# A two-layer hybrid trunk on one core: decay rows in fewer transfers, a new instruction list for the second layer, and a shortened last block

## The chip, the cores and the metric

The kernel runs on one core of one Trainium2 chip. The metric is the device time of one execution in microseconds; lower is better. Before the change the median of three timed runs is 1061.02 us (1060.3 to 1061.82). Besides these there is one profiled execution, from which all rows of this document come.

## The reference

The program is one inference step of a trunk with two layers, on 128 prompt tokens and 512 sample tokens of width 1024, in float32. Each layer does a pre-RMSNorm, a shift and scale from a conditioning vector, a mixer branch and a gated residual add; a last RMSNorm follows. Layer 0's mixer is a convolution branch. Layer 1's mixer, where the whole change lies, is a bidirectional Mamba-2 scan:

```
u = h @ w_in
z, xbc, dt_raw = split(u)
xbc = silu(depthwise_conv(xbc, 5 taps))
xs, bm, cm = split(xbc)            # 32 heads of 64, 4 groups of state 128
dt = softplus(dt_raw + dt_bias)
y_f, s_f = ssd_scan(xs, dt_f, a_f, bm, cm, h0_f)              # chunks of 128 tokens
y_b, s_b = ssd_scan(flipped, ..., h0_b)
y = (y_f + flip(y_b) + d * xs) * silu(z)
y = rms_norm(y, per group of 512) * norm_g
out = y @ w_out
x = x + gate * out
result = rms_norm(x, final_norm_g)
```

Inside the scan each chunk needs the matrix `exp(a_cum[l] - a_cum[s])` (the decays) of each head, the product `C B^T`, and the states that are carried from chunk to chunk in both directions. The outputs are both token groups after the last norm, and the prompt's two final states.

## The kernel before

The 640 tokens are five chunks of 128: chunk 0 is the prompt, chunks 1 to 4 the sample. Each matrix product is split in three: activations and weights have a high and a low part in a reduced float32 format, and high by high, low by high and high by low are added in PSUM. So each weight tile is loaded (SyncE's queue, L1250), cast to its high part on ACT (L1255, or L1258 with the norm's gain folded in for the out-projection), and subtracted to its low part on DVE or POOL (L1264, L1267).

Nothing of the order is left to chance. The order of each engine's instructions is made by a list scheduler when the program is built (class `Order`, L247 and after). Work is written as generators that yield one operation at a time: its engine, an assumed duration, the call, and for a DMA the time that its bytes take. The scheduler keeps a clock for each engine and one for the transfers; it takes the operation that can start first, a priority from a table (`PRIO0` for layer 0, `PRIO1` for layer 1) breaking ties. A DMA with a byte time lands 0.3 us after its issue, plus the byte time, plus 2.2 us; TensorE's operations are placed `run.lead` after what they wait for. Ring buffers (`RB1`: xs, st, gf, gb and others) limit how far it can run ahead. What the scheduler decides is the order on each engine; on the chip the instructions wait for semaphores in that order. A wrong assumption therefore shows as an engine that waits while work behind it is ready.

Layer 1's backbone is `PLAN1`, a list of 45 tiles: x, b, c and z tiles of four groups (each 128 output columns over 640 tokens, 48 matmuls, L1307), and "o" pieces, the out-projection of a group's half (60 matmuls, L1558). Group 3's out-projection is not in the list: its weights come after the list's last tile (`out_weights`, L1862) and its products stand in `last_products` (L1901, matmuls L1913), which takes chunk after chunk, both halves of 512 columns, and starts a chunk only when all four weight tiles are there. After z33, the last z tile, SiLU (L1428, L1429), a gate product (L1787), a high and low split (L1811, L1816) and the sum of squares (L1829, L1833, L1834, L1839) stand before these products.

Between the layers, `first_steps` and `first_x` (L2084, L2093) empty the PSUM banks of the time steps and of the first two x tiles: most copies go to ACT (L1337, L1338, L2087, L2088).

The scan of a group (`group`, L1606) starts when B and all four x tiles of the group are there. For every chunk, `decays` (L1585) loads two tiles of decay rows from a table in DRAM that was written once: gb with 512 and gf with 1024 columns. The rows of the two directions come from different rows of the table, so partitions 0 to 63 and 64 to 127 have a transfer each: four transfers (L1599 twice, L1602 twice), each repeating one row of DRAM over 64 partitions. `decay` then subtracts on POOL (L1575), selects on DVE (L1577) and takes exponentials on ACT (L1581). Chunk states, their decay and their use are at L1633, L1638, L1652, L1666, L1701, L1705 and L1707; the products of decays and x at L1769.

The end: `last_residual` takes a product out of PSUM (L1924), adds it to x (L1927) and squares it with a running sum (L1928). `final` adds the sums of both halves (L1935), takes root and reciprocal (L1936, L1937); `final_half` scales and stores (L1951, L1953, L1955), `gained_half` has multiplied the first half by the norm's gain on POOL before (L1944).

Of the kernel before, what the change touches and what calls it, by code (L numbers as in the profile page):

```python
# [7 lines left out]
F32 = mybir.dt.float32  # L8
# [5 lines left out]
P = 128  # L14
# [29 lines left out]
PRIO1 = {"lead": -2, "sq_way": 2, "add_way": -3, "squares": -7, "room": -5, "roots": -2, "turn_x": 4, "gate_rows": 0, "gate_loads": -6, "residual": -5, "last_products": 3, "last_residual": 7, "final": 4, "gained_half": -5, "low": 1, "x_after": -4, "filler": 7, "decay_half": 5, "decay_state": 1, "chain0": -6, "chain1": 5, "other_y": 0, "copy_y": 7, "split_y": -1, "groups": 2, "decays": 0, "norms": 5, "gate": 6, "products1": 1, "products0": -7, "residual0": 0, "final0": -4, "w_chain": 3, "time_steps": 1, "columns": -5, "logarithm": 5, "rows_out": -3, "ends_out": 2, "weights_out": -6, "first_steps": 3, "b_after": 0, "c_after": 3, "z_after": -5, "split": 0, "add_residual": -5, "out_weights": -5, "free_bc": -4, "final1": -3, "prompt": -7, "residual1": 1, "store": 6, "final_rest": -4}  # L44
PLAN1 = "z00 b0 c0 z01 x02 x03 x13 b1 x10 x12 x22 x11 z02 x20 c1 x23 z03 b2 z10 x21 o00 z11 x33 o01 z12 z13 z20 c2 z30 x30 z21 x32 o10 z22 c3 z23 z31 o11 b3 x31 o20 z32 o21 z33"
RB1 = {"xs": 2, "st": 7, "gf": 2, "gb": 1}
# [5 lines left out]
def trunk(ctx: ExitStack, tc: tile.TileContext, a: dict):  # L52
# [1130 lines left out]
    if True:  # L1183
# [61 lines left out]
        def w_load(i, src, g=None):  # L1245
# [22 lines left out]

            def split():
                yield get("wh")  # L1270
# [29 lines left out]
        def dense_steps(ps, wh, wl, tiles, wofs, banks):  # L1300
# [12 lines left out]
        def project(i, name):  # L1313
            yield key(("w", i))
            yield get("mm")
            ps = mm(name)
            t = yield from dense_steps(ps, *W[i], h, [k * 128 for k in range(KD)], EVEN)
# [14 lines left out]
        def evacuate(ps):  # L1332

            ups.sort()
            u = up[ups.pop(0)[1]]
            if isinstance(ps, tuple):
                return u, tuple(lambda o=o, a0=a0, a1=a1: [S.copy(out=u[:, o + b * (a1 - a0) : o + (b + 1) * (a1 - a0)], in_=z_[:, a0:a1]) for b, z_ in enumerate(ps)] for o, a0, a1 in ((2, 0, 64), (132, 64, HN)))  # L1337
            return u, (lambda: S.copy(out=halves(u[:, 2:130]), in_=ps[:, :, 0:64]), lambda: S.copy(out=halves(u[:, 132:644]), in_=ps[:, :, 64:HN]))  # L1338

        def convolve(ps, j, tag, bufs, name, cell, u=None):  # L1340
            if u is None:
                yield get("up")
                u, copies = evacuate(ps)
                yield op(ACT, 0.27, copies[0])
                t = yield op(ACT, 0.6, copies[1])
# [150 lines left out]
        def gate_loads():  # L1496
            yield key(("gated",))
            for g in range(3):
                for hf in range(2):
# [7 lines left out]
                    t = yield op(SP, 0.9, load, 1.3)  # L1507
# [12 lines left out]
            t = yield op(SP, 1.8, load_last, 2.6)  # L1520
# [64 lines left out]
        def decays():  # L1585
            yield key(("cols",))
            for g in range(NG):
                for n, ch in enumerate(ORDER[g]):
# [4 lines left out]
                    def load():  # L1593
# [3 lines left out]
                        for i in range(2):  # L1597
                            r, col = at(1 - i, ch, 8 * g)
                            nc.sync.dma_start(out=gb[64 * i : 64 * i + 64], in_=acb[col // 128, i, r : r + 8, :].rearrange("h n -> (h n)").unsqueeze(0).broadcast_to([64, 512]))  # L1599
                        for i in range(2):  # L1600
                            r, col = at(i, ch, 8 * g)
                            nc.sync.dma_start(out=gf[64 * i : 64 * i + 64], in_=acf[col // 128, r : r + 8, :].rearrange("h n -> (h n)").unsqueeze(0).broadcast_to([64, 1024]))  # L1602
# [647 lines left out]
```

## Time and profile before

| what | value |
|---|---|
| timed runs, median (three) | 1061.02 us |
| the profiled execution's own time | 1060.24 us |
| its span, first to last instruction | 1058.3 us |
| mean granted TensorE clock | 0.995 |
| TensorE busy | 1032.8 us |
| VectorE (DVE) busy | 825.9 us |
| ScalarE (ACT) busy | 667.1 us |
| GpSimd (POOL) busy | 442.1 us |

The span is what the profile's rows count from and to; the execution's own time has 1.9 us around it. "Busy" of TensorE counts matmuls whose ends are modelled and which overlap, so 98% does not mean that the array works at its peak. Layer 1's first products of `PLAN1` start at 545.09 us, so the change concerns the second half of the span. A row of a chain or a timeline gives start and length in us, the engine, the line and the tiles; an "x" behind it is a count of instructions merged into it.

### The profile page before, as it was taken

The page shows a single profiled execution, that of the slowest core. Times are in us where ns is not written, and L with a number is a line of the kernel's source. Part 1 is how long each engine was busy: PE and PEld are TensorE (multiplying, and loading weights), DVE is VectorE, ACT ScalarE, POOL GpSimd, SP SyncE. Part 2 cuts the span into 40 slices and gives each one's busy share as a digit, 9 for nine tenths or more (in the row PEclk, how much of TensorE's full clock was granted, in tenths as well). Part 3 has the DMA queues.
Part 4 walks back from the last instruction along what each step waited for, and adds up shares of the span by engine and source line. Part 5 has one row for each costly group of instructions (what it writes and reads, how often), then busy time and mean ns, then how long its engine had stood idle before and what let it go on. Part 6 is the DMA issues. An engine that isn't in the chain of part 4 may idle for free.

```text
span 1058.3 us, 19181 instructions
## 1 busy us (share of the span) xinstructions
PE 1032.8 (98%) x7485; PEld 947.5 (90%) x7485; DVE 825.9 (78%) x1240; ACT 667.1 (63%) x1112; POOL 442.1 (42%) x443
## 2 busy tenths in 40 slices
PE   7999999999999999999999999999999999999986
PEld 4999999999999999999999988897879888998765
DVE  3589999998997689102678879889888687687897
ACT  6458788778687678433577666686556444572464
POOL 0029989978596511111000056334522644003642
PEclk9999999999999999999999999999999999999989
DMA  9598888788766667776222443334325344224513
GB/s 357 201 266 198 193 215 196 180 209 219 180 136 135 133 144 153 145 165 148 61 61 83 117 127 96 121 109 129 101 78 142 100 130 136 65 80 144 144 42 100
DMA packets 64362, 151.82 MB, mean 143 GB/s; under 512 B 9472, under 2 KB 22416, under 8 KB 64272
## 3 DMA queue, kind: packets, MB, share of 16 engines
q1 hardware_dynamic: 52480, 118.35, 36.0%
q0 software_dynamic: 8640, 30.94, 17.5%
q10 hardware_dynamic: 3152, 1.31, 0.5%
q8 instruction: 59, 0.97, 0.4%
q14 instruction: 31, 0.25, 0.1%
HBM read 145.45 MB, written 5.12 MB: 142 GB/s over the span
## 4 chain that ended last, share of the span: by engine, by line
PE 82%; DVE 6%; POOL 4%; ACT 4%; issue 2%; DMA 1%; SPq 1%; POOLq 0%; DVEq 0%; ACTq 0%
PE pz L1307 9%; PE xs L1307 8%; PE o L1558 8%; POOL cv L887 4%; PE o L1913 3%; PE po L1701 2%; PE B L1307 2%; PE C L1307 2%; PE pst L1638 2%; PE py L1769 2%; DVE cva L815 2%; PE o__4964 L158 1%; PE o__5273 L158 1%; PE o__5244 L158 1%; PE o__4954 L158 1%
## 5 line engine op out<-in xcount | busy, mean ns | idle before, releaser
L815 DVE SCALAR_TENSOR_TENSOR cva<-v,cst,cva 128x550 f32<-128x550 f32 (+12 forms) x346 | 270.3, 824 | 12.2 <-ACT cva L807 7.1
L887 POOL TENSOR_TENSOR cv<-cv,tp 128x490 f32<-128x490 f32 (+5 forms) x134 | 172.8, 1289 | 8.5
L846 ACT ACTIVATE tp<-v,cst 128x490 f32<-128x490 f32 (+5 forms) x134 | 92.5, 718 | 36.3 <-POOL cv L887 36.0
L425 ACT CAST wh<-wf 128x1024 fp32r<-128x1024 f32 x63 | 65.9, 1046 | 63.0 <-PE o__5273 L158 29.9
L1307 PE MATMUL pz<-h_hi,wh 128*128 128x320 f32 x256 | 86.3, 337 | 1.7 <-ACT up L1338 1.7
L1707 POOL TENSOR_TENSOR y<-y,yo 128x512 f32<-128x512 f32 x32 | 49.7, 1553 | 83.0 <-DVE yo L1705 79.3
L1307 PE MATMUL pz<-h_hi,wl 128*128 128x320 f32 x256 | 79.1, 309 | 0.0
L1307 PE MATMUL pz<-h_lo,wh 128*128 128x320 f32 x256 | 79.0, 309 | 0.0
L1307 PE MATMUL xs<-h_hi,wh 128*128 128x320 f32 x224 | 76.4, 341 | 0.0
L1351 DVE SCALAR_TENSOR_TENSOR xs<-up,cst,xs 128x642 f32<-128x642 f32 x64 | 65.7, 1028 | 10.2 <-ACT xs L1349 8.8
L1581 ACT ACTIVATE gf<-gf,cols 128x128 f32<-128x128 f32 x160 | 50.7, 391 | 29.8 <-DVE gf L1577 29.7
L1307 PE MATMUL xs<-h_hi,wl 128*128 128x320 f32 x224 | 69.3, 309 | 0.0
L1307 PE MATMUL xs<-h_lo,wh 128*128 128x320 f32 x224 | 69.1, 308 | 0.0
L435 ACT ACTIVATE wl<-wh 128x1024 fp32r<-128x1024 f32 x58 | 61.6, 1061 | 1.7
L1575 POOL TENSOR_TENSOR gb<-gb,cols 128x512 f32<-128x512 f32 x20 | 25.8, 1290 | 88.1 <-DMA gb<-acb 85.6
L1264 DVE TENSOR_TENSOR wl<-wf,wh 128x1024 fp32r<-128x1024 f32 x38 | 50.9, 1345 | 15.1 <-ACT wh L1255 15.1
L436 POOL DMA_DIRECT2D wl<-w_in x43 | 37.5, 872 | 54.8 <-ACT wl L435 54.2
L1307 PEld LDWEIGHTS pz<-h_hi,wh 128*128 128x128 f32 x256 | 48.1, 188 | 5.6 <-issue 3.4
L1558 PE MATMUL o<-wh,yh 128*128 128x512 f32 x120 | 53.2, 443 | 0.0
L1255 ACT CAST wh<-wf 128x1024 fp32r<-128x1024 f32 x38 | 39.6, 1047 | 18.1 <-DMA wf<-w_xbc 6.1
L1307 PEld LDWEIGHTS pz<-h_lo,wh 128*128 128x128 f32 x256 | 48.2, 188 | 3.1 <-issue 2.9
L436 POOL DMA_DIRECT2D wl<-w_out x15 | 13.0, 865 | 90.4 <-ACT wl L435 90.4
(848 smaller groups left out, 3500.4 us busy)
## 6 DMA issues: line engine op xcount, KB each, us to landing
wf<-w_in SPq DMA_DIRECT2D x48, 512.0 KB, 3.9
wl<-w_in POOLq DMA_DIRECT2D x43, 512.0 KB, 6.6
wa<-w_ada SPq DMA_DIRECT2D x64, 256.0 KB, 6.0
wf<-w_out SPq DMA_DIRECT2D x32, 512.0 KB, 3.6
wf<-w_xbc SPq DMA_DIRECT2D x24, 512.0 KB, 3.7
gf<-acf SPq DMA_DIRECT2D x40, 256.0 KB, 4.3
wa<-w_ada SPq DMA_DIRECT2D x16, 512.0 KB, 10.7
wf<-w_z SPq DMA_DIRECT2D x16, 512.0 KB, 3.7
```

What stands on the lines that cost most here:

```text
L425: t = yield op(ACT, 1.05, lambda: S.copy(out=wh, in_=wf))
L435: yield op(ACT, 1.06, lambda: S.activation(out=wl, in_=wh.bitcast(F32), func=AF.Copy, scale=-1.0))
L436: t = yield op(PD, 0.7, lambda: G.dma_start(out=wl, in_=src, accum_op=ALU.add))
L815: t = yield op(VE, 0.24 + 0.01 * (hi - lo), lambda: V.scalar_tensor_tensor(out=rows64(accs[i], lo, hi), in0=rows64(vs[i], lo + d, hi + d), ...
L846: t = yield op(ACT, 0.72, lambda: S.activation(out=tp[:, :, 0 : hi - lo], in_=rows64(vs[i], lo + d, hi + d), func=AF.Copy, scale=w_dw(i, t ...
L887: t = yield op(PO, 1.3 + 0.019 * (hi - lo - 49), lambda: G.tensor_add(out=rows64(cv[i], lo, hi), in0=rows64(cv[i], lo, hi), in1=sgs["tp", ...
L1264: e_.tensor_sub(out=cell["wl"], in0=cell["wf"], in1=cell["wh"].bitcast(F32))
L1307: T.matmul(ps[:, b, at_ : at_ + t1 - t0], lhsT=w_, rhs=t_[:, t0:t1], start=k == 0 and n == 0, stop=k == nk - 1 and n == 2)
L1351: t = yield op(VL, 0.97, lambda: V.scalar_tensor_tensor(out=acc, in0=u[:, d : d + PW], scalar=c("w_c", j * 5 + d), in1=acc, op0=ALU.mult, ...
L1558: T.matmul(ps, lhsT=t_, rhs=w_, start=k == 0 and n == 0, stop=k == 3 and n == 2)
L1581: t = yield op(ACT, 0.39, lambda: S.activation(out=gv[:, h_, :], in_=gv[:, h_, :], func=AF.Exp, bias=cols1[ch][:, o8 + h_ : o8 + h_ + 1]), ...
L1707: t = yield op(PO, 1.29, lambda: G.tensor_add(out=y, in0=y, in1=yo))
```

## The change

All of it lies in layer 1.

- **Tables.** `PLAN1`, `PRIO1` and `RB1` get new values. Two xs buffers become three, seven st buffers six.
- **Seam.** The first weight tile is cast in two halves, each subtracted on its own, and the first products of the first tile need the first half alone. The copies out of PSUM at the seam may go to DVE instead of ACT. The lead before TensorE's operations is 0.3 us up to the seam's end; after it `0.2 * (lead + 7)` with lead -4 (0.6 us) where it was -2 (1.0 us).
- **Decay rows.** Two transfers per chunk: one for gb and one for gf, each with a source pattern of two directions, times 64 repeats, times the row.
- **Landings.** The scheduler's byte times of several loads are changed: decays, gates, states and the chunk ends.
- **Late out-projection of group three.** Two of its four weight tiles are loaded with the list's weights and two by a generator of their own after z33. The products of each chunk and half are a chain of their own and need only that half's weights. The last chunk's second half is done in two pieces of 256 columns.
- **Final root.** The first sums are scaled and given epsilon ahead, and serve as the bias of the root.

```
-PLAN1 = "z00 b0 c0 z01 x02 x03 x13 b1 x10 x12 x22 x11 z02 x20 c1 x23 z03 b2 z10 x21 o00 z11 x33 o01 z12 z13 z20 c2 z30 x30 z21 x32 o10 z22 c3 z23 z31 o11 b3 x31 o20 z32 o21 z33"
-RB1 = {"xs": 2, "st": 7, "gf": 2, "gb": 1}
+PLAN1 = "x03 x02 x23 z00 b0 c0 z01 x10 b1 z02 x12 x13 z03 x11 x20 c1 z10 x21 c2 z11 x32 o00 x22 o01 z12 b2 z13 z20 c3 z21 x31 o10 z22 x30 o11 z23 x33 z30 b3 z31 o20 z32 z33 o21"
+RB1 = {"xs": 3, "st": 6, "gf": 2, "gb": 1}
...
             def split():
+                if i == 0:
+                    yield get("wh")
+                    yield get("wl")
...
+                    for n in range(2):
+                        t = yield op(ACT, 0.62, lambda: S.copy(out=cell["wh"][:, n * 512 : n * 512 + 512], in_=cell["wf"][:, n * 512 : n * 512 + 512]))
+                        start(first_half(n, t), t)
+                    return
...
                 for k, (hi, lo) in enumerate(tiles):
+                    if late and b == 0 and k == 4:
+                        yield key(late)
...
-                        for i in range(2):
-                            r, col = at(1 - i, ch, 8 * g)
-                            nc.sync.dma_start(out=gb[64 * i : 64 * i + 64], in_=acb[col // 128, i, r : r + 8, :].rearrange("h n -> (h n)").unsqueeze(0).broadcast_to([64, 512]))
-                        for i in range(2):
-                            r, col = at(i, ch, 8 * g)
-                            nc.sync.dma_start(out=gf[64 * i : 64 * i + 64], in_=acf[col // 128, r : r + 8, :].rearrange("h n -> (h n)").unsqueeze(0).broadcast_to([64, 1024]))
-                    t = yield op(SP, 1.5, load, 2.2)
+                        r, col = at(0, ch, 8 * g)
+
+                        def two(rows):
+                            v = rows.rearrange("(i p) n -> i p n", i=2)[:, r : r + 8, :].rearrange("i h n -> i (h n)")
+                            return v.unsqueeze(1).broadcast_to([2, 64, v.shape[1]])
+
+                        for t_, rows in ((gb, acb[col // 128].rearrange("f p n -> (f p) n")[64:192]), (gf, acf[col // 128])):
+                            nc.sync.dma_start(out=t_, in_=two(rows))
+                    t = yield op(SP, 1.1, load, 2.8)
...
-                t = yield op(SP, 0.45, load, 0.8)
+                t = yield op(SP, 0.45, load, 1.4)
...
+        def late_weights():
+            yield key(("z", 3, 3))
+            for n in range(2):
...
+                yield op(SP, 0.35, load, 1.35)
+                for k in range(2):
...
+                    yield op(ACT, 0.62, lambda: S.activation(out=wh, in_=wf, func=AF.Copy, scale=sn))
+                    t = yield op(VL, 0.72, lambda: V.scalar_tensor_tensor(out=wl, in0=wf, scalar=sn, in1=wh.bitcast(F32), op0=ALU.mult, op1=ALU.subtract))
...
-        def last_products():
-            for ch in LAST:
-                yield key(("split", 3, ch), *[("w3", n) for n in range(4)])
+        def last_products(ch, hf):
+            yield key(("split", 3, ch), ("w3", 2 * hf), ("w3", 2 * hf + 1))
...
+        def pieces(ch, hf):
+            return ((0, 256), (256, 512)) if (ch, hf) == (LAST[-1], 1) else ((0, 512),)
...
         def final(ch):
-            yield key(("fin", ch, 0), ("fin", ch, 1), ("fgb",))
-            r = fin[:, ch, 2:3]
-            yield op(VE, 0.15, lambda: V.tensor_add(out=r, in0=fin[:, ch, 0:1], in1=fin[:, ch, 1:2]))
-            yield op(ACT, 0.24, lambda: S.activation(out=r, in_=r, func=AF.Sqrt, scale=1.0 / 1024, bias=epsb), "sqrt")
+            r = fin[:, ch, 3:4]
+            n = len(pieces(ch, 1))
+            yield key(("fin", ch, 0, 0))
+            yield op(VE, 0.16, lambda: V.tensor_scalar(out=r, in0=fin[:, ch, 0:1], scalar1=1.0 / 1024, scalar2=EPS, op0=ALU.mult, op1=ALU.add))
+            if n > 1:
+                yield key(("fin", ch, 1, 0))
+                yield op(VE, 0.16, lambda: V.scalar_tensor_tensor(out=r, in0=fin[:, ch, 1:2], scalar=1.0 / 1024, in1=r, op0=ALU.mult, op1=ALU.add))
+            yield key(("fin", ch, 1, n - 1), ("fgb",))
+            yield op(ACT, 0.24, lambda: S.activation(out=r, in_=fin[:, ch, n : n + 1], func=AF.Sqrt, scale=1.0 / 1024, bias=r), "sqrt")
...
         def first_steps():
...
+                yield either((ACT, 0.27, lambda: take0(S)), (VE, 0.25, lambda: take0(V)), bias=0.1 * PRIO1["dt_way"])
...
         def first_x(j):
...
-            yield op(ACT, 0.27 + 0.2 * j, copies[0])
-            z_ = yield op(ACT, 0.6 + 0.2 * j, copies[1])
+            yield either((ACT, 0.27 + 0.2 * j, lambda: copies[0](S)), (VE, 0.25 + 0.15 * j, lambda: copies[0](V)), bias=0.1 * PRIO1["x_way"])
+            z_ = yield either((ACT, 0.6 + 0.2 * j, lambda: copies[1](S)), (VE, 0.67 + 0.1 * j, lambda: copies[1](V)), bias=0.1 * PRIO1["x_way"])
...
-            run.lead = 0.2 * (PRIO1["lead"] + 7)
+            run.lead = 0.3
...
             run.run(("begun",))
+            run.lead = 0.2 * (PRIO1["lead"] + 7)
...
-            start(last_products(), 0.0)
+            start(late_weights(), 0.0)
+            for ch in LAST:
+                for hf in range(2):
+                    start(last_products(ch, hf), 0.0)
```

More of the change, by code (lines that the diff above doesn't have):

```diff
@@ L1297, in w_free, with dense_steps @@
             put("wl", t)
-        def dense_steps(ps, wh, wl, tiles, wofs, banks):
+        def dense_steps(ps, wh, wl, tiles, wofs, banks, late=None):
             nk = len(tiles)
@@ L1316, in project @@
             ps = mm(name)
-            t = yield from dense_steps(ps, *W[i], h, [k * 128 for k in range(KD)], EVEN)
+            t = yield from dense_steps(ps, *W[i], h, [k * 128 for k in range(KD)], EVEN, None if i else ("w", 0, "b"))
             w_free(i, t)
@@ L1343, in convolve @@
                 u, copies = evacuate(ps)
-                yield op(ACT, 0.27, copies[0])
-                t = yield op(ACT, 0.6, copies[1])
+                yield op(ACT, 0.27, lambda: copies[0]())
+                t = yield op(ACT, 0.6, lambda: copies[1]())
                 put("mm", t)
@@ L1519, in load_last @@
                         gate_in(gts[3, hf][cd], cd, 4 * hf, 4)
[L1520 removed]
+            t = yield op(SP, 1.9, load_last, 4.2)
             post(("gt", 3), t)
@@ L1925, in last_residual, with as_x @@
             put("mm", t)
-            x_ = xv(ch, hf)
-            t = yield either((VL, 0.66, lambda: V.tensor_add(out=x_, in0=x_, in1=as_part(tmp, ch))), (PO, 1.29, lambda: G.tensor_add(out=x_, in0=x_, in1=as_part(tmp, ch))), bias=0.2)
-            t = yield op(ACT, 0.62, lambda: S.activation(out=as_part(tmp, ch), in_=x_, func=AF.Square, accum_out=fin[:, ch, hf : hf + 1]))
+            x_ = xs_[:, 4 * hf + c0 // 128 : 4 * hf + c1 // 128, :]
+            x_ = part(x_, ch)
+            def as_x(z_):
+                return z_.rearrange("p (j n) -> p j n", n=128) if half else as_part(z_, ch)
@@ L1929, in last_residual @@
+            if half:
+                t = yield op(VL, 0.42, lambda: V.tensor_add(out=x_, in0=x_, in1=as_x(tmp)))
+            else:
+                t = yield either((VL, 0.66, lambda: V.tensor_add(out=x_, in0=x_, in1=as_x(tmp))), (PO, 1.29, lambda: G.tensor_add(out=x_, in0=x_, in1=as_x(tmp))), bias=0.2)
+            t = yield op(ACT, 0.4 if half else 0.62, lambda: S.activation(out=as_x(tmp), in_=x_, func=AF.Square, accum_out=fin[:, ch, hf + n : hf + n + 1]))
             put("yo", t)
-            post(("fin", ch, hf), t)
+            post(("fin", ch, hf, n), t)
@@ L1938, in final @@
+            t = yield op(VE, 0.14, lambda: V.reciprocal(out=fin[:, ch, 4:5], in_=r))
             start(final_half(ch, 0), t, "final")
@@ L1941, in gained_half @@
         def gained_half(ch, hf):
-            yield key(("fin", ch, hf), ("fgb",))
+            yield key(*[("fin", ch, hf, n) for n in range(len(pieces(ch, hf)))], ("fgb",))
             x_ = xv(ch, hf)
@@ L1947, in final_half @@
         def final_half(ch, hf):
-            x_, r = xv(ch, hf), fin[:, ch, 3:4]
+            x_, r = xv(ch, hf), fin[:, ch, 4:5]
             if hf == 0:
@@ L1967, in trunk @@
         n_items = len(items)
-        for n in range(3):
-            items.append((None, a["w_out2"][3, n], 12 + n % 2 * 2))
+        for n in range(2):
+            items.append((None, a["w_out2"][3, n], 12 + n * 2))
         def filler():
```

102 lines of the change are left out of this document (59 added, 43 removed).

## The prediction

> **What bounds the kernel now.** I read the page's busy times first, then busy time by window of 20 us over the whole span, then TensorE's waits and the chain that ended last, and last the timeline at the places they pointed to.
>
> ```profile
> PE 1032.8 (98%) x7485; PEld 947.5 (90%) x7485; DVE 825.9 (78%) x1240; ACT 667.1 (63%) x1112; POOL 442.1 (42%) x443
> ```
>
> TensorE is the bound by share, but its 98% hides where it isn't. In the windows below the columns are busy us (instructions) of PE, its weight loads, DVE, ACT and POOL, then granted clock, DMA share and GB/s.
>
> ```profile
> 540.00:560.00 20.00, 18.29 (x130) 17.95 (x129) 13.36 (x16) 15.51 (x30) 0.71 (x4) 1.00 0.36 107
> 720.00:740.00 20.00, 18.42 (x102) 13.70 (x101) 18.66 (x31) 12.49 (x26) 9.62 (x7) 1.00 0.45 123
> 920.00:940.00 20.00, 20.00 (x115) 17.68 (x113) 16.93 (x34) 11.50 (x23) 0.00 (x0) 1.00 0.15 51
> 980.00:1000.00 20.00, 20.00 (x100) 15.49 (x95) 16.35 (x20) 7.25 (x15) 12.54 (x11) 1.00 0.50 133
> 1000.00:1020.00 20.00, 15.58 (x79) 10.28 (x79) 18.42 (x42) 13.75 (x27) 10.52 (x8) 0.83 0.36 106
> 1020.00:1040.00 20.00, 19.59 (x98) 14.75 (x97) 18.99 (x40) 12.32 (x31) 11.31 (x8) 1.00 0.10 27
> ```
>
> After the first weights have arrived TensorE loses time mainly at four places: 1.71 us at the seam between the layers (540:560), 1.58 us in 720:740, 4.42 us in 1000:1020, and all that follows its last matmul. In 1000:1020 the granted clock is 0.83 besides, so up to (1 - 0.83) x 20 = 3.4 us of array time more: about 7.8 us together, the largest loss of layer 1. POOL stands still in 920:940, and DVE has only 1.6 and 1.0 us left in the last two windows. Elsewhere a faster helper engine buys nothing.
>
> The chain that ended last leaves TensorE exactly there (start, length, what):
>
> ```profile
> 940.28 6.26 PE xs L1307 x42
> 774.56 9.09 PE o L1558 x39
> 987.28 3.92 DMA gf<-acf
> 1001.61 1.23 ACT wh L1258 x2
> 1002.84 1.46 ACT gf L1581 x5
> 1004.30 0.93 ACT L1428
> 1012.12 1.97 PE py L1769 x16
> 1026.16 1.02 PE py L1769 x16
> ```
>
> The list of layer 1 ends "b3 x31 o20 z32 o21 z33". Group 3's scan needs all its x tiles, and x31 ends at 940.28 + 6.26 = 946.54; POOL, which does the scan's weighting, is idle until then. z33 comes last, so its SiLU (behind weight casts, decays and a table load on ACT, 1001.61 to 1004.30), the gate and the split stand before the out-projection of group 3 with only scan remnants for TensorE. The sixteen products of L1769 take 1.97 us at 1012 and 1.02 at 1026: that is the half clock.
>
> The Trainium skill ("TensorE: Matmul & The Clock Gate", the section on the warmup mystery) says that the gate halves the clock after an idle window of about 3.4 us and needs about as long to open. The trace differs in size: TensorE's longest single wait there is shorter, as the timeline has it in a later sentence, and the clock fell all the same. Taken by the page alone the 3.4 us would not have been lost, and the end term below would be smaller by that.
>
> **The change, part by part.** The sums go against the profiled execution, 1060.24 us with a span of 1058.3; the median of the three timed runs is 1061.02, 0.78 higher, and I add that at the end.
>
> Seam.
>
> ```profile
> 542.39 1.99 ACT L1255 CAST wh<-wf 128x1024 fp32r<-128x1024 f32 x2 [2.16 <-PE dt L1051]
> 543.07 0.31 PE L1051 MATMUL xs<-h_hi,wl 128*128 128x320 f32 x1
> 544.29 0.74 ACT L1338 COPY up<-xs 128x128 f32<-128x128 f32 x2
> 545.09 0.41 PE L1307 MATMUL pz<-h_hi,wh 128*128 128x320 f32 x1 [1.71 <-ACT up L1338]
> 1009.63 0.56 PE L1839 MATMUL ssp<-ones,ysq 128*128 128x1 f32 x2 [2.07 <-DVE ysq L1834]
> ```
>
> TensorE waits for a PSUM bank that ACT empties only after two full weight casts (1.99 us). The change casts the first weight tile in halves, splits it on DVE or POOL, starts the products on the first half, and lets DVE take the copies. The last of the products of L1051 ends at 543.38; a copy of 0.74 started then ends at 544.1, against 545.03 now: 0.9 us gained. Bounds: 1.71 gained if nothing is waited for, 0.3 lost if the second half of the split comes late (each half's four k steps cover only 12 products). The last row shows TensorE's longest wait near the clock's fall, 2.07 us.
>
> Decay rows. Four transfers a chunk become two of double size, 20 chunks.
>
> ```profile
> 985.51 1.08 SPq L1599 DMA_DIRECT2D gb<-acb  x2
> L1599 SPq DMA_DIRECT2D gb<-acb x40: 444/547/1073, 602.0 to 1002.5; - x40
> L1602 SPq DMA_DIRECT2D gf<-acf x40: 444/590/1622, 603.2 to 1005.7; - x40
> wf<-w_out SPq DMA_DIRECT2D x16, 512.0 KB, 4.1
> fgb<-fg_row SPq DMA_DIRECT2D x1, 512.0 KB, 4.8
> q1 hardware_dynamic: 21983, 45.42, 38.5%
> ```
>
> Now the first issue is at 985.51 and the last row lands at 987.28 + 3.92 = 991.20: 5.69 us. SyncE is freed of two issues of 0.55 to 0.59 us a chunk, 23 us in all, spread over 400 us: nothing by itself. A 512 KB load lands in 4.1 to 4.8 us by the nearest rows, so the pair would land 0.55 + 4.1 to 4.8 = 4.7 to 5.4 us after the first issue: 0.3 to 1.0 sooner. This is on the path only where the chain shows the load, at 987, so it goes into the end term and isn't added. The list's own due time for the pair becomes 0.3 + 2.8 + 2.2 = 5.3 us, inside this. The price if the transfers are spread badly is a rival below.
>
> End of the list. It becomes "x33 z30 b3 z31 o20 z32 z33 o21". Group 3's last input is now b3, with five pieces of work behind it as x31 had four: one z tile more, 48 products at 6.26 / 42 = 0.149 us, 7.2 us. From x31's end to the end of TensorE's work (1050.14, where the tail's first row starts) there are 103.6 us, of which 4.42 + 0.41 are idle and up to 3.4 lost to the clock: 8.2. If the scan's chain keeps its length, 7.2 of these are filled. And z33 now has o21 behind it, 60 products at 9.09 / 39 = 0.233 us = 14.0 us, which covers casts, table load, SiLU and gate (1001.61 to 1009.6, 8 us). If that cover fails, the 8 us stay. What is late next is DVE: it keeps its work (18.42 and 18.99 of 20 us) and o21's five residuals join it there. I take 4.5 us gained, nearer to 7.2 than to nothing because POOL stood idle while it waited for x31; bounds 7.2 gained, 3 lost (DVE's 1.6 + 1.0 us of room used up and missed).
>
> Late weights. One more w_out load with two casts and two subtractions now waits for z33's SiLU. On SyncE it stands behind decay loads; ACT pays 1.23 for its two casts, DVE 1.5 for two 512-wide steps of 0.76 as in the tail's rows. It serves second halves only, and the first halves no longer wait for it (they are ten separate chains instead of one). Covered by o21's 14.0 us; uncovered it costs 4.1 + 1.2 + 1.5 = 6.8 us once. I count nothing.
>
> Tail, in order on the chain.
>
> ```profile
> 1050.14 0.76 DVE tmp L1924
> 1050.93 0.71 DVE x L1927
> 1051.66 0.73 ACT tmp L1928 x2
> 1051.66 0.63 ACT L1928 ACTIVATE tmp<-x 128x512 f32<-128x512 f32 x1 [1.31 <-DVE x L1927]
> 1052.41 0.17 DVE fin L1935
> 1052.60 0.30 ACT fin L1936
> 1053.19 0.72 ACT x L1951
> 532.96 0.48 DVE L1123 SCALAR_TENSOR_TENSOR modo<-x,gsc,rs 128x256 f32<-128x256 f32 x1
> 1007.78 0.42 DVE L1833 TENSOR_TENSOR ysq<-ysq 128x256 f32<-128x256 f32 x1
> 538.21 0.51 ACT L1129 ACTIVATE h_hi<-modo,mod 128x256 fp32r<-128x256 f32 x1 [0.43 <-DVE modo L1123]
> ```
>
> The last block's second half goes in pieces of 256 columns. By the 256-wide rows tmp falls from 0.76 to 0.48, the add from 0.71 to 0.42, the square by 0.63 - 0.51 = 0.12 or a little more, and the sum at L1935 (0.17 and a hop of 0.02) leaves the path since the other pieces' sum is already in the root's bias: 0.28 + 0.29 + 0.12 + 0.19 = 0.88. TensorE pays: on the line from 0.149 at 320 to 0.233 at 512 columns a 256-wide product takes 0.12 us, 24 x 0.12 - 12 x 0.233 = 0.1. Net 0.8 gained; bounds 1.0 and 0.3 (if the extra PSUM bank is waited for).
>
> The rest of the order. All priorities, the list's other 38 places, TensorE's lead (1.0 to 0.6 us), xs buffers 2 to 3, st 7 to 6. No row prices it. It can win the 1.58 us of 720:740 and the few tenths of its neighbours, 2.3 at most; it can lose as much again as layer 1 now loses outside the end, about 4. I take 0, with both ends kept.
>
> Sum: -0.9 - 4.5 - 0.8 = -6.2. Profiled: 1060.24 - 6.2 = 1054.0; against the median, 1061.02 - 6.2 = 1054.8.
>
> **The rivals.** *DVE takes TensorE's place at the end.* For it: 18.42 and 18.99 of 20 us busy, and no DVE work is removed there but 0.17 us a chunk. Against: DVE has 3.65 us free in 980:1000, where group 3's scan can now begin earlier. Only seam and tail remain: 1061.02 - 1.7 = 1059.3.
>
> *The new loads run on few DMA engines*, the slower case. The new source pattern's outermost dimension is 2, where it was 64, and if the work is divided by that dimension, two engines carry it. In 602 to 1003 us the q1 row's packets take 0.385 x 16 x 401 = 2470 engine-us for 45.42 MB, 18.4 KB a us. A chunk's 786 KB over two engines is 393 KB each, 21.4 us, against a pitch of (1005.7 - 602.0) / 20 = 20.2 us a chunk: from about 20 us on the loads set the pace. Twenty take 427 us from 602, and 52.6 us follow the last now: 1082 us of span. The same engines' share of all other loads, (45.4 - 15.7) MB / 16 / 18.4 = 101 us, would make it 1183; middle about 1130. Against it stands only the list's due time of 5.3 us; no row shows such a pattern.
>
> The Trainium skill ("DMA: Bandwidth & Descriptors", the sections on the semaphore's 16 and the rules for kernel authors) states this division: the number of engines must divide the outermost dimension of both sides, so a leading 2 confines a transfer to two. No run here shows it yet; by that rule this rival is the case.
>
> *The new order stalls TensorE in mid-layer*, with a lead of 0.6 us where 1.0 stood and x23's buffer held from the start of the list until group 2's first x tile: 4 us lost there and the end gains half, 1061.02 - 1.7 - 2.2 + 7 = 1064. Against: one xs buffer more.
>
> *The change does not do what it says*: were z33's SiLU still listed behind casts and decays, 1059 again; it goes with the first rival.
>
> **How the numbers follow.** Forecast 0.66, DVE 0.14, two engines 0.13, mid-layer stalls 0.07. A measurement of this kernel can tell 0.2%, 2.1 us, from no change. Faster: the forecast and about half of DVE's case (under 1058.9), 0.73. Within: the other half, 0.07. Slower: 0.20. The forecast's bounds are 1061.02 - 1.7 - 7.2 - 1.0 - 2.3 = 1048.8 below; above, the range takes in DVE's case and the first of the mid-layer losses, to 1062. It leaves out the two-engine case and part of the stalls.
>
> **What would show it.** Right: the gap before the first product of layer 1 near 0.8 us; z33's SiLU under o21's products; granted clock 1.00 until TensorE's last product; no fin sum on the last chain, whose DVE steps read 0.48 and 0.42; gf loads of 512 KB landing in 4 to 5 us. Wrong: gf landing over 10 us, with TensorE waiting for decays or weights all through layer 1; PE idle over 3 us in one window of 560 to 980; or the last 50 us with DVE full and TensorE still at 16 of 20.

## The result, and the profile after

| kernel | median us | ratio to the kernel before, 95% interval |
|---|---|---|
| before | 1060.5 (five runs) | 1 |
| after the change | 1208.6 (1203.7 to 1209.3, five runs) | 1.1385 [1.1368, 1.1401] |

The change makes the kernel 148 us slower. The forecast was 1054.8 us with a range up to 1062; the rival that the new loads run on few DMA engines, with a chance of 0.13 and a price of 1082 to 1183 us of span, came true, and was priced too low even at its upper end (the span is 1207.0 us).

The page of the changed kernel (span 1207.0 us, mean clock 0.942): busy times, then the chain that ended last, by engine.

```profile
PE 1069.3 (89%) x7497; PEld 976.4 (81%) x7497; DVE 808.0 (67%) x1250; ACT 667.8 (55%) x1110; POOL 434.8 (36%) x444
PE 64%; DMA 24%; DVE 7%; issue 2%; ACT 1%; SPq 1%; POOL 0%; DVEq 0%; ACTq 0%; POOLq 0%
```

TensorE's share is down from 98% to 89%, and no engine has taken its place: all of them stand idle more. A transfer has: 24% of the chain is DMA, where it was 1% in the kernel before. The windows of after, columns as in the prediction:

```profile
540.00:560.00 20.00, 18.07 (x128) 17.46 (x128) 17.48 (x25) 14.66 (x27) 0.23 (x3) 1.00 0.34 108
860.00:880.00 20.00, 8.43 (x41) 8.16 (x41) 4.82 (x6) 6.84 (x14) 2.75 (x2) 0.66 0.39 109
980.00:1000.00 20.00, 7.92 (x34) 7.09 (x34) 5.36 (x11) 6.19 (x14) 3.01 (x3) 0.66 0.39 120
1142.00:1146.60 4.60, 4.60 (x30) 2.77 (x28) 4.53 (x12) 2.17 (x4) 0.49 (x1) 1.00 0.13 51
```

Up to the seam (540:560) TensorE fares much as before. From the first decay loads on, TensorE is idle for more than half of some windows in which it was full before, and its clock falls to 0.66 there. The last row shows what the loads do. In this stretch practically nothing but the last pair of decay loads moves: the DMA share is 0.13, and 2 of 16 engines are 0.125. The two engines move 51 GB/s, so a chunk's 786 KB take about 786 / 51 = 15.4 us, an estimate that the text uses from here on. The kernel before, in the chain's stretch at 987, where such a pair lands beside other loads:

```profile
987.50:990.50 3.00, 3.00 (x12) 1.80 (x10) 1.52 (x3) 1.66 (x4) 1.26 (x2) 1.00 0.94 241
```

Share 0.94 and 241 GB/s: nearly all sixteen are at work. The Trainium skill ("DMA: Bandwidth & Descriptors", the rules for kernel authors) says that an outermost dimension smaller than 16 confines the whole transfer to at most that many engines; the trace agrees, with its 0.13 for a leading 2.

Who waits for it: first the waits of after (us in total, times, longest), then its issues of the two loads (ns min/median/max, first and last start), then the chain of waits in 849 to 892.

```profile
DVE gf L1599 <- DMA gf<-acf: 126.6, 14, 14.2
POOL gb L1597 <- DMA gb<-acb: 49.3, 12, 14.8
ACT L1603 <- DMA gf<-acf: 25.3, 6, 9.3
```
```profile
L1626 SPq DMA_DIRECT2D gb<-acb x20: 501/507/635, 606.9 to 1139.2; - x20
L1626 SPq DMA_DIRECT2D gf<-acf x20: 484/490/498, 607.6 to 1140.2; - x20
```
```profile
849.54 0.77 DVE gf L1599
850.31 0.02 SPq L1626
...
850.37 0.51 SPq L1626
...
850.97 19.51 DMA gf<-acf
...
870.60 0.72 DVE gf L1599
...
871.93 0.74 DVE gf L1599
872.67 0.02 SPq L1626
...
872.72 0.51 SPq L1626
...
873.28 17.84 DMA gf<-acf
```

The chain reads as a cycle: DVE has read gb, SyncE issues the next pair at once, the pair lands 19.5 us later (its own 15.4; the rest is probably the share of other loads that these two engines carry, which no row here separates), DVE reads it, SyncE issues the next, 17.8 us. Against that stands a landing of 3.9 us before. The pace of the chunks follows: from the first gb issue to the last there are 19 steps, (1139.2 - 606.9) / 19 = 28.0 us each, where it was (1002.5 - 602.0) / 19 = 21.1. So 532.3 - 400.5 = 131.8 of the 148.7 us by which the span grew lie between the first and the last decay load; 4.9 lie ahead of the first load (606.9 - 602.0) and 1207.0 - 1139.2 - (1058.3 - 1002.5) = 12.0 behind the last.

### The profile page after: what moved, and what is told of

Same layout as the page of the kernel before. It is cut to its first block, busy times and chain, and to the rows that moved or that the text cites. A ratio compares the mean times of both kernels' runs of the same rounds, so it can differ in the third digit from the quotient of the medians.

```text
span 1207.0 us, 19094 instructions
## 1 busy us (share of the span) xinstructions
PE 1069.3 (89%) x7497; PEld 976.4 (81%) x7497; DVE 808.0 (67%) x1250; ACT 667.8 (55%) x1110; POOL 434.8 (36%) x444
## 4 chain that ended last, share of the span: by engine, by line
PE 64%; DMA 24%; DVE 7%; issue 2%; ACT 1%; SPq 1%; POOL 0%; DVEq 0%; ACTq 0%; POOLq 0%
DMA gf<-acf 18%; PE pz L1327 5%; PE xs L1327 4%; DMA o_st<-stp 3%; PE o L1580 2%; PE o L1940 2%; PE C L1327 2%; DMA st_b<-st_b 2%; DVE gf L1599 1%; PE pst L1662 1%; PE o__4964 L158 1%; PE o__5273 L158 1%; PE o__5244 L158 1%; PE o__5264 L158 1%; PE o__5251 L158 1%
## 5 line engine op out<-in xcount | busy, mean ns | idle before, releaser
L1599 DVE COPY_PREDICATED gf<-msk,gb 64x512 f32<-64x512 int32 x40 | 30.5, 762 | 132.8 <-DMA gf<-acf 126.6
L425 ACT CAST wh<-wf 128x1024 fp32r<-128x1024 f32 x63 | 65.9, 1046 | 63.4 <-PE o__5273 L158 30.0
L1327 PE MATMUL pz<-h_hi,wh 128*128 128x320 f32 x256 | 90.9, 355 | 3.3 <-DVE tmp L1555 3.3
L1327 PE MATMUL xs<-h_hi,wh 128*128 128x320 f32 x224 | 82.5, 368 | 0.9 <-ACT up L1357 0.9
L1327 PE MATMUL pz<-h_lo,wh 128*128 128x320 f32 x256 | 82.2, 321 | 0.0
L1373 DVE SCALAR_TENSOR_TENSOR xs<-up,cst,xs 128x642 f32<-128x642 f32 x64 | 61.7, 965 | 11.2 <-ACT xs L1371 10.1
L1676 POOL TENSOR_TENSOR stn<-st_f,decb 128x512 f32<-128x512 f32 x4 | 4.8, 1206 | 164.0 <-DMA st_f<-st_f 164.0
L1580 PE MATMUL o<-wh,yh 128*128 128x512 f32 x120 | 58.3, 486 | 0.0
L1725 PE MATMUL po<-stn,C 128*128 128x512 f32 x48 | 28.7, 687 | 28.5 <-DVE stn L1690 24.8
L1752 PE MATMUL pty<-cst,y 128*128 128x128 f32 x80 | 14.8, 316 | 43.7 <-POOL y L1731 43.7
```

The lines of the kernel that those rows point to most:

```text
L425: t = yield op(ACT, 1.05, lambda: S.copy(out=wh, in_=wf))
L1327: T.matmul(ps[:, b, at_ : at_ + t1 - t0], lhsT=w_, rhs=t_[:, t0:t1], start=k == 0 and n == 0, stop=k == nk - 1 and n == 2)
L1373: t = yield op(VL, 0.97, lambda: V.scalar_tensor_tensor(out=acc, in0=u[:, d : d + PW], scalar=c("w_c", j * 5 + d), in1=acc, op0=ALU.mult, ...
L1580: T.matmul(ps, lhsT=t_, rhs=w_, start=k == 0 and n == 0, stop=k == 3 and n == 2)
L1599: t = yield op(VL, 0.75, lambda: V.copy_predicated(out=gv[r, :, r], mask=msk[r].unsqueeze(1).broadcast_to([64, 8, 64]), data=bv[r]))
```

## Experiments: the two loads

Theory A: the two transfers on two engines each are the whole loss, and it follows the time that their packets take. Theory B: the loss is in the new order (list, priorities, buffers), and the loads only show it. The expectations name a third, "form": a merged transfer of double size with the repeat in the middle is slow, whatever its outermost dimension.

**The change with the four transfers of before (after_four).**

```
-                        for t_, rows in ((gb, acb[...][64:192]), (gf, acf[col // 128])):
-                            nc.sync.dma_start(out=t_, in_=two(rows))
+                        for i in range(2):
+                            r, col = at(1 - i, ch, 8 * g)
+                            nc.sync.dma_start(out=gb[64 * i : 64 * i + 64], in_=acb[...].broadcast_to([64, 512]))
+                        ...(gf the same way)
```

> The changed kernel with the decay rows in four transfers a chunk again; the list, the priorities and all else as changed. Two engines (the source pattern's outermost 2 confines each load to two DMA engines, and that alone costs the time): 1054.8 us by the forecast's sum, 1049 to 1060, granted clock 1.00 from 620 to 1000. New order (list, priorities and lead cost the time): about 1205, as the change. Form (one transfer of double size with the repeat in the middle is slow, whatever its outermost dimension): 1054.8 too.

Measured: 1061.08 us, ratio 1.0003 [0.9994, 1.0012]. All of the 148 us is gone. But the forecast's 1054.8 isn't reached either: the rest of the change is worth nothing together that could be told (0.1% either way).

**The kernel before with the two transfers (before_two).** The same lines the other way round, in the kernel before.

> The kernel before with the two transfers of the change, its own list, priorities and assumed landings kept. Two engines: the loads set the pace here too; 20 chunks at the 21.4 us of the prediction and their neighbours on the same engines, 1180 to 1230 us. New order: 1060.5, within 3. Form: 1180 to 1230 as well.

Measured: 1212.01 us, 1.1425 [1.1409, 1.144]. The old order loses as much as the new one. Theory B is out.

**More parts in the source pattern (after_k16, after_k8, after_k4).** The leading dimension 2 becomes 16, 8 or 4, the bytes and the number of transfers stay. These three kernels leave out the right decays: the loads fetch rows of other chunks, and the exponential takes a constant in their place, so that all decays are one. They serve to time the transfers alone. With 4 parts:

```
-                t = yield op(ACT, 0.39, lambda: S.activation(out=gv[:, h_, :], in_=gv[:, h_, :], func=AF.Exp, bias=cols1[ch][:, o8 + h_ : o8 + h_ + 1]), "exp")
+                t = yield op(ACT, 0.39, lambda: S.activation(out=gv[:, h_, :], in_=gv[:, h_, :], func=AF.Exp, scale=0.0, bias=epsb), "exp")
...
-                            v = rows.rearrange("(i p) n -> i p n", i=2)[:, r : r + 8, :].rearrange("i h n -> i (h n)")
-                            return v.unsqueeze(1).broadcast_to([2, 64, v.shape[1]])
+                            v = rows.rearrange("(i p) n -> i p n", i=4)[:, r % 32 : r % 32 + 8, :].rearrange("i h n -> i (h n)")
+                            return v.unsqueeze(1).broadcast_to([4, 32, v.shape[1]])
```

> As the run with 4 rows, with 16 rows times 8 repeats; decays all one again. Two engines: sixteen engines carry it, within 5 us of the run with four transfers, and a little faster if fewer issues on SyncE's queue are worth anything. Form: the repeat is still in the middle and the transfer still of double size, about 1205. New order: about 1205.

> The change with its two transfers over 8 rows times 16 repeats; the rows are those of other chunks and the decays all one, as in the runs with 4 and 16 rows. Few engines: a chunk's two loads take 3.9 us of each of eight engines, where 15.4 (two engines) cost 148 us and 7.7 (four) 52; on the line through these two, which meets the time without loss at 3.6 us, about 4 us: 1064, 1060 to 1072. A cost of the pattern itself: it would not fall with the number of rows, over 1100.

> The change with the same two transfers, but their source pattern runs over 4 rows times 32 repeats instead of 2 times 64; the rows are those of other chunks, and the exponent takes a constant in their place, so the decays are all one. Two engines: four engines carry it, at 0.159 us for 4 KB and 0.084 us for 2 KB a packet 7.8 us of each a chunk, under the 20 us of the pace; loads still land later than the list assumes: 1060 to 1110, about 1075. New order or form: about 1205.

Measured: 1060.12 us (0.9994 [0.9985, 1.0003]) with 16 parts, 1072.68 (1.0113 [1.01, 1.0127]) with 8, 1112.66 (1.0485 [1.0467, 1.0504]) with 4. So one transfer for both directions costs nothing in itself, and the theory of the form is out, since the run with 16 parts has the same form. What costs is how few parts lead it. Where little but after_k4's last pair moves, the DMA share is 0.26, and 4 of 16 engines are 0.25:

```profile
1052.00:1060.00 8.00, 8.00 (x46) 5.42 (x45) 7.93 (x18) 4.05 (x7) 2.14 (x2) 1.00 0.26 97
```

The runs with 8 and 4 parts are dearer than I expected, each just above its range. With 8, I had thought that the list's slack would hide about 4 us of landing, and it hides only part of it.

**One load of the two (before_two_gf).** Before, with gf merged and gb in two transfers. Does the packet time or a loop set the pace? In the loop, the one gb buffer ties each pair to DVE's reading of the pair before (the cycle above).

> Before, with only the forward rows in one transfer; the backward rows stay in two. Packet time on the two engines per chunk: 10.2 us of the forward rows and 0.7 us of the backward ones, against 15.5 us with both. If the excess follows the packet time of the two engines as between the runs with four and with two repeated parts (52 us at 7.7, 148 us at 15.4), 1150 us (1140 to 1160). If the loop through the one buffer of the backward rows carries the loss (their load must land behind the forward rows of the chunk before, and holds the next pair), it is broken here, and the time is 1070 to 1110 us. If the forward rows alone set the pace, 1195 us or more.

Measured: 1147.88 us, 1.0829 [1.0813, 1.0846]. That is the value by packet time (1150), not the 1070 to 1110 of the loop. The five doses together (the fourth in the order of before, the others in the new one), with the time on each engine scaled from the 15.4 us measured on two, the first and last issue of gb (of gf where gb has two transfers), and the pace from them:

| kernel | us per chunk on an engine | first and last issue | pace, us | median, us |
|---|---|---|---|---|
| after_k16 | 1.9 | 607.5, 995.8 | 20.4 | 1060.1 |
| after_k8 | 3.9 | 606.4, 1008.9 | 21.2 | 1072.7 |
| after_k4 | 7.7 | 607.2, 1049.8 | 23.3 | 1112.7 |
| before_two_gf | 10.3 + 0.6 | 603.5, 1087.3 | 25.5 | 1147.9 |
| after | 15.4 | 606.9, 1139.2 | 28.0 | 1208.6 |

From 3.9 us on the pace rises by 0.5 to 0.7 us for each us of packet time ((23.3 - 21.2) / 3.8 = 0.55; (25.5 - 23.3) / 3.2 = 0.7; (28.0 - 25.5) / 4.5 = 0.56), with no threshold at the chunk's own 20 us, which the rival had assumed. Why it is some 0.6 and not 1 is only argued: the list can run part of its work while a pair is late.

**A second gb buffer (before_two_gb2) and its control (before_two_st6).** To break the loop itself:

```
-RB1 = {"xs": 2, "st": 7, "gf": 2, "gb": 1}
+RB1 = {"xs": 2, "st": 6, "gf": 2, "gb": 2}
```

> The kernel before with the two transfers, and two gb buffers instead of one (six st buffers instead of seven to make room). Loop theory (with two engines the pace of 28 us a chunk is a loop: a load of 15.4 us of packets, then subtract and select, and only then is the single gb buffer free for the next load): the next chunk's gb load runs under the selection, the pace falls towards the engines' own 15.4 us plus about 6 us of the other loads' share, 20 x 4 to 7 us less than the 1212 of the run with one buffer: 1070 to 1140. Rate theory (the two engines' queue is full, whatever the buffers): 1205 to 1215.

Measured: 1233.36 us, 1.1632 [1.1614, 1.1649]: slower, which neither theory had. But a state tile had to make room for the buffer, so the run changed two things. Its control has st 6 and gb 1.

> Before with the two transfers, and one state tile less (six for seven) at one buffer of the backward rows: the control of the run with two buffers, which also had six. If the second buffer itself made that run slower (its loads come earlier and lie ahead of weight loads on the two engines), the tile is worth little here: 1208 to 1218 us. If the missing tile was the cost, 1228 us or more, and then the second buffer did nothing or little. In between, both.

Measured: 1224.04 us, 1.1541 [1.1525, 1.1557]. So the missing state tile costs 12.0 us of the 21.4 and the second buffer the other 9.3: in between, as the expectation's last words allowed. Issues of gb, control first:

```profile
L1600 SPq DMA_DIRECT2D gb<-acb x20: 485/512/642, 601.4 to 1148.8; - x20
```
```profile
L1600 SPq DMA_DIRECT2D gb<-acb x20: 501/508/4481, 601.0 to 1156.6; - x20
```

The control's pace is 28.8 us, as before_two's (601.2 to 1146.9, 28.7); its loss lies behind the last load, 1221.9 - 1148.8 = 73.1 us against 1208.7 - 1146.9 = 61.8. With the second buffer the pace is 29.2: no faster. The cycle in the chain is real, but nearly all of it (19.5 of 22.4 us from issue to issue) is the transfer, and a second buffer can't shorten that. Why it makes things worse stays open. Some waits for other loads are longer (ACT for the z weights 25.0 us against 17.8 in the control, and 11.0 for x, b or c weights where the control has none), which fits decay packets queued earlier in front of them on the two engines, but no run took that apart.

## Experiments: the rest of the change

The base here is after_four. Its windows, and its rows at the seam:

```profile
540.00:560.00 20.00, 18.07 (x129) 17.47 (x128) 17.33 (x25) 14.49 (x27) 0.38 (x3) 1.00 0.34 108
680.00:720.00 40.00, 39.78 (x280) 38.17 (x280) 37.73 (x54) 35.85 (x70) 8.81 (x6) 1.00 0.37 119
1000.00:1020.00 20.00, 19.11 (x76) 12.54 (x75) 19.79 (x33) 8.98 (x17) 9.13 (x7) 1.00 0.33 99
1020.00:1040.00 20.00, 17.75 (x96) 14.50 (x97) 19.44 (x51) 12.77 (x29) 6.87 (x6) 1.00 0.20 53
```
```profile
543.51 0.75 DVE L2135 TENSOR_SCALAR room<-dt,cst 32x128 f32<-32x128 f32 x2
543.91 0.41 PE L1327 MATMUL xs<-h_hi,wh 128*128 128x320 f32 x1 [0.85 <-ACT up L1357]
544.27 0.49 DVE L2144 TENSOR_SCALAR room<-dt,cst 32x256 f32<-32x256 f32 x1
544.79 1.29 DVE L1271 TENSOR_TENSOR wl<-wf,wh 128x512 fp32r<-128x512 f32 x2
545.54 0.41 PE L1327 MATMUL xs<-h_hi,wl 128*128 128x320 f32 x1 [1.08 <-DVE wl L1271]
```

**The seam (four_dt).** The first gap is 0.85 us, as forecast (0.8), but a second of 1.08 follows: DVE, which took the copies of the time steps (L2135), subtracts the low half too late. The copies are put back on ACT, and the first weight tile's half steps get another priority:

```
-PRIO1 = {"first_x": -7, "first_half": -1, "dt_way": 5, ...}
+PRIO1 = {"first_x": -7, "first_half": -9, "dt_way": 50, ...}
```

> The run with four transfers, the copies of the time steps at the seam kept on ACT (in that run DVE took them, and the low half of the first weight tile came late behind them, a second gap of 1.1 us); the scheduler's choices later shift with it. Seam theory: TensorE's gaps at the seam fall from 1.9 to about 0.9 us; the rest of the list is reshuffled, whose bound is the 2 us by which layer 1's middle differed between lists so far: 1060, 1058 to 1063. If the seam doesn't matter: 1061, within 2, with the gaps as they were.

Measured: 1059.31 us, 0.9989 [0.9981, 0.9998]. Its windows:

```profile
540.00:560.00 20.00, 19.15 (x137) 18.78 (x135) 15.78 (x20) 16.27 (x31) 0.04 (x1) 1.00 0.26 83
680.00:720.00 40.00, 38.56 (x280) 37.89 (x279) 35.50 (x50) 32.08 (x59) 6.25 (x5) 1.00 0.37 112
```

The second gap is gone: TensorE is idle 20 - 19.15 = 0.85 us at the seam, 0.86 less than before, which is the forecast's 0.9. But in 680:720 it is idle 1.44 us where after_four lost 0.22. What was won at the seam is given back 140 us later. By how much the median gains, if at all, is at the limit of what can be told.

**z33 last again (four_z33).** Is it o21 behind z33 that covers the SiLU, the gate and the late weights?

```
-PLAN1 = "... b3 z31 o20 z32 z33 o21"
+PLAN1 = "... b3 z31 o20 z32 o21 z33"
```

> The run with four transfers, the list ending 'z32 o21 z33' as before the change instead of 'z32 z33 o21'. Cover theory (o21 behind z33 hides z33's SiLU, gate and split; that closed the hole of 1000 to 1020): the hole comes back, 3 to 8 us more, 1064 to 1069, and a granted clock under 1 before TensorE's end. DVE theory: DVE does the same work in the same stretch, 1061, within 1.5.

Measured: 1067.84 us, 1.0067 [1.0054, 1.008], 6.8 us more than after_four.

```profile
1000.00:1020.00 20.00, 16.13 (x107) 12.43 (x105) 17.69 (x34) 10.34 (x21) 9.02 (x8) 1.00 0.37 106
1020.00:1040.00 20.00, 15.40 (x55) 12.13 (x56) 17.59 (x46) 9.05 (x21) 5.59 (x4) 0.75 0.08 26
```

TensorE loses 2.98 + 2.35 us more than in after_four's two windows, and the clock falls to 0.75. The cover that the forecast named is real, and so is the price when it is gone.

**The last blocks in strict order (four_chain).** One generator for the ten blocks, chunk by chunk, where the change has ten:

```
-        def last_products(ch, hf):
-            yield key(("split", 3, ch), ("w3", 2 * hf), ("w3", 2 * hf + 1))
+        def last_products():
+            for ch, hf in [(c_, h_) for c_ in LAST for h_ in range(2)]:
+                yield key(("split", 3, ch), ("w3", 2 * hf), ("w3", 2 * hf + 1))
```

> The run with four transfers, and the ten last blocks of group 3 taken chunk after chunk, first half then second, as before the change, instead of as ten chains that the scheduler may interleave; pieces, bias and late weights stay. Order theory (in the run with four transfers the last two blocks on TensorE belong to two chunks, so that two norms and four stores fall together behind the end, 10.2 us from TensorE's end to the span's against 8.2 before): the part behind TensorE's end falls to about 7.4, 1058.3 us. DVE theory (DVE, at 19.4 of 20 us in the last windows, sets the end whatever the order): 1061, within 1.

Measured: 1066.76 us, 1.0057 [1.0045, 1.0069].

```profile
1020.50 0.50 PE L1941 MATMUL o<-wl,yh 128*128 128x512 f32 x1 [0.73 <-DVE wl L1267]
1030.44 0.38 PE L1863 MATMUL ssp<-ones,ysq 128*128 128x1 f32 x2 [3.44 <-ACT ss L1871]
```

Neither forecast holds. Each chunk's first half now stands behind the second half of the chunk before; TensorE waits for a weight's low part (0.73) and, later, 3.44 us at once for ACT. In ten separate chains other blocks can go first during such waits. Nor does the part behind TensorE's end fall to 7.4: TensorE's last product ends at 1055.96, so it takes 1065.0 - 1055.96 = 9.0 us, although the two pieces and one chunk's norm now stand alone at the very end. DVE is scaling another chunk there, for 1.82 us from 1055.48 beside POOL's product, and the last short step waits for it until 1057.29.

**The last chunk alone held back (four_last).** Only its two blocks wait for the chunk before. The aim is that one norm and not two stands at the very end:

```
-            yield key(("split", 3, ch), ("w3", 2 * hf), ("w3", 2 * hf + 1))
+            yield key(("split", 3, ch), ("w3", 2 * hf), ("w3", 2 * hf + 1), *([("lp", LAST[-2], n) for n in range(2)] + [("lp", ch, 0)] * hf if ch == LAST[-1] else []))
```

> The run with four transfers, where only the last chunk of group 3 is held back: its first half is placed when both halves of the chunk before it are placed, its second half after its first; the other eight blocks stay free. Order theory in its narrow form (the two last chunks' norms and stores fall together; holding all ten blocks in order lost it because first halves then wait behind second halves for the late weights): 2 us less behind TensorE's end, 1059.1, 1058 to 1060. DVE theory: 1061, within 1.

Measured: 1059.93 us, 0.9997 [0.9988, 1.0005]; its span is 1057.6 where after_four's is 1057.8. Nothing that can be told, and the trace says why: the order at the end is the same. In both kernels two whole blocks, 24 products of 512 columns, stand between the last chunk's two pieces (here from 1040.13 to 1045.73), and ACT still scales two chunks at the end, at 1050.32 and 1051.56. Those two blocks belong to a chunk that the edit does not hold: the last chunk in the list waits for the one before it, but the products of yet another come between its own two pieces. So this run did not test the forecast.

**The last half block whole (four_whole).** Without the two pieces of 256 columns:

```
-            return ((0, 256), (256, 512)) if (ch, hf) == (LAST[-1], 1) else ((0, 512),)
+            return ((0, 512),)
```

> The run with four transfers, the last chunk's second half whole again instead of in two pieces of 256; nothing else. Order theory: the second piece is the last block there, so without pieces the last chain gets 0.5 to 0.9 us longer, 1061.6 to 1062. DVE theory: two instructions fewer on a full engine, 1060.3 to 1061.

Measured: 1059.81 us, 0.9998 [0.999, 1.0007]. The pieces win nothing. Why is seen in after_four's last microseconds:

```profile
1046.78 1.27 POOL L1987 TENSOR_TENSOR x<-x,fgb 128x512 f32<-128x512 f32 x1 [3.77 <-ACT tmp L1966]
1047.06 1.54 DVE L1965 TENSOR_TENSOR x<-x,tmp 128x512 f32<-128x512 f32 x1
1047.36 0.28 PE L1940 MATMUL o<-wl,yh 128*128 128x256 f32 x1
1048.52 0.47 DVE L1955 SCALAR_TENSOR_TENSOR tmp<-o,rs,gt 128x256 f32<-128x256 f32 x1
1049.02 0.42 DVE L1963 TENSOR_TENSOR x<-x,tmp 128x256 f32<-128x256 f32 x1
1050.53 0.72 ACT L1994 ACTIVATE x<-x,fin 128x512 f32<-128x512 f32 x1
1051.77 0.72 ACT L1994 ACTIVATE x<-x,fin 128x512 f32<-128x512 f32 x1 [0.52 <-DVE fin L1980]
```

TensorE's last product ends at 1047.64, but the short steps (0.47 and 0.42, as forecast) start only at 1048.52: DVE is still in the add of another chunk, which takes 1.54 us beside POOL's product. And two chunks' norms come out together, with two scalings on ACT (1050.53 and 1051.77). With the block whole, TensorE's last product ends 0.8 us later, at 1048.47, and the span is still 1057.5 against 1057.8.

**Both small ones (last_dt).** four_dt and four_last in one kernel.

> The change with four transfers, with the copies of the time steps left on ScalarE and the last chunk's two blocks held behind the blocks of the chunk before. If the two gains add (1.7 us and 1.1 us under the change with four transfers, 1061.1 us), 1058.2 us; if VectorE paces the end whatever comes ahead of it, the first gain is taken back there and the time is 1059.3 us (1058.8 to 1060).

Measured: 1059.14 us, 0.9988 [0.9979, 0.9997], as four_dt alone (1059.31). There was no second gain to add, since four_last's edit leaves the end's order as it was here too. This is the best version found, about 0.1% under the kernel before, less than a measurement of this kernel can safely tell.

## Why the prediction was wrong

**Decay rows: the step that failed.** The prediction let the pair land 4.7 to 5.4 us after the first issue, priced by other loads of 512 KB, and so put the loads at nothing in its sum. The nearest rows were near in size and not in shape: they load weights and gains whose pattern leads with 128 partitions; this pattern leads with 2. In the rows shown gf landed 17.8 and 19.5 us after its own issue, which is 18.4 and 20.1 us after the pair's first (850.37 and 872.72). The rival beside it had the right mechanism, and its weight of 0.13 had no row against it but the list's own due time, which is an assumption of the program and not a measurement. The rule of the Trainium skill ("DMA: Bandwidth & Descriptors", the rules for kernel authors) spoke for it and nothing measured spoke against it, so it should have been the likeliest case.

**The rival's price.** Its 21.4 us of transfer were too many (15.4 by the measured rate): 18.4 KB a us and engine is the rate over a stretch in which all engines have work, while these two move 51 GB/s, 25.5 KB a us each. Its rule, that the loads cost only from 20 us a chunk on, was wrong the other way: with 7.7 us the kernel already loses 52. The two errors did not cancel; its middle of 1130 us of span was 77 us too low.

**Seam: forecast -0.9.** The first gap became 0.85 us as worked out; the second half of the split was late, which the text had named as its bound of 0.3 lost. The sum of the gaps is 1.93 where it was 1.71: 0.2 us lost. With the copies on ACT the -0.9 was there (0.85), and was lost again by 720.

**End of the list: forecast -4.5.** From before to after_four TensorE's last product ends 2.5 us earlier (1050.10 to 1047.64). Of that 0.3 is layer 0 (its last product ended at 543.06 here, 543.38 before), and the seam and the middle take 0.2 each: the end gave about 2.5, inside its bounds and well under the value taken. The cover by o21 was right (four_z33), and the clock stayed at 1.00 where it had been 0.83. What kept the gain small is, by the traces, the rival "DVE takes TensorE's place": DVE is busy 19.79 + 19.44 = 39.23 of 40 us in 1000 to 1040, where it had 37.41, and in after_four the chain that ended last runs on DVE alone (its waits included) from 988.5 to 1024.3, where before it went over a load, ACT, DVE and TensorE. No run took work off DVE there to test it.

**Late weights: forecast 0.** Right as the change stands: in after_four TensorE has no wait for them after 995 us. In four_chain, once the ten chains are one, there is one of 0.73 us.

**Tail: forecast -0.8.** From TensorE's last product to the span's end it takes 1057.8 - 1047.6 = 10.2 us, where it took 1058.3 - 1050.1 = 8.2: 2.0 lost. The short pieces have the forecast lengths. The sum took the last block alone, and left out what else DVE and ACT have to do then: the blocks of two chunks now end together, and DVE is late for the short steps. Strict order, with one chunk alone at the end, still needs 9.0 (four_chain), and four_last did not change the order; so what would mend it is open.

**Rest of the order: forecast 0.** Over 560 to 960 TensorE is busy 397.6 us in after_four and 397.7 before. The number is right, but by two errors that cancel: 2.1 us are won from 680 to 760, where the prediction saw the hole of 1.58, and 0.4 and 1.8 are lost in 560 to 680 and 760 to 960, where TensorE had been full.

Without the loads the terms make -0.3 (layer 0) + 0.2 + 0.2 - 2.5 + 2.0 = -0.4 us; after_four's span against before's is -0.5 (1057.8 and 1058.3).

## What to carry to other kernels

Before two transfers are merged, look at the leading dimension of the merged pattern: here a leading 2 put both on two of sixteen engines, and 786 KB took about 15.4 us; the kernel lost 148 us with 2 parts, 52 with 4, 12 with 8, and nothing with 16. A row of equal bytes prices a transfer only if its pattern leads alike, and a due time in a scheduler is no evidence. When TensorE gets work earlier near the end, see first how many us another engine has free there; here VectorE had 2.6 of 40 before.

## What the runs showed of the hardware

- In these stretches an engine that ran nearly alone moved more than one of many: 51 GB/s on two engines is 25.5 each, and 97 on after_k4's four is 24, where sixteen at a share of 0.94 moved 241, 16 each. Other loads were among the last, and why it is less is not shown.
- In after_four, DVE's add of 128x512 took 1.54 us when it began behind POOL's product (1046.78 to 1048.05), and 0.69 at 1045.25 with POOL idle. The short last step waited for it. In four_whole it was POOL that took longer: the add began first (1046.77) and took 0.69, and POOL's product of 1046.91 took 1.70 instead of 1.27.
- The clock fell in two ways. First after, through one wait of TensorE of 11.57 us that began at 862.23, by windows of 4 us:

```profile
860.00:864.00 4.00, 2.23 (x15) 1.97 (x14) 0.00 (x0) 0.00 (x0) 0.00 (x0) 1.00 0.36 113
864.00:868.00 4.00, 0.00 (x0) 0.00 (x0) 0.00 (x0) 0.00 (x0) 0.00 (x0) 0.74 0.58 162
868.00:872.00 4.00, 0.00 (x0) 0.00 (x0) 1.36 (x3) 0.00 (x0) 0.00 (x0) 0.50 0.61 151
```

  A mean of 0.74 over 4 us with half clock at its end means that it fell about (0.74 - 0.5) / 0.5 x 4 = 1.9 us into the window, at 865.9, 3.7 us after the wait began: near the 3.4 us of the Trainium skill ("TensorE: Matmul & The Clock Gate", the warmup mystery). But in four_z33, by the records, it fell without so long a wait:

```profile
1020.00:1024.00 4.00, 1.36 (x7) 0.88 (x7) 4.00 (x6) 2.19 (x4) 2.77 (x2) 0.88 0.39 131
1024.00:1028.00 4.00, 3.53 (x12) 3.03 (x13) 3.93 (x12) 1.86 (x5) 0.06 (x1) 0.50 0.00 0
```

  TensorE is busy 1.36 of 4 us there, with waits of 1.41 and 1.53 us among a few matmuls, and in the kernel before the longest wait near the fall was 2.07 us. A few short matmuls between waits did not keep the clock up there.
